# A decoder step on one core: the first conditioning section, loaded and computed in quarters

## The chip, the core and the metric

The kernel runs on one core of a Trainium2 chip. Its time is the device time of one execution in microseconds (us). TensorE (PE) multiplies, VectorE (DVE) and ScalarE (ACT) work on tiles, GpSimd (POOL) issues a few small transfers and SyncE (SP) issues nearly all the others. Each engine takes its instructions in the order in which they stand in its queue, and an instruction that waits holds up those behind it.

## What is computed

Two layers of a decoder trunk, for a prompt of 512 rows and for 8 samples of 4 rows, 544 columns in all once the rows are turned into columns. Cut to what the change touches:

```python
mod = jax.nn.silu(c) @ w + b                        # c: 1 + 8 rows of 1024; w: 1024 x 6144
sh_m, sc_m, g_m, sh_f, sc_f, g_f = split(mod, 6)    # six sections of 1024 features
hin = rmsnorm(x, norm_g[layer, 0]) * (1.0 + sc_m) + sh_m
gate_br, x_br = jnp.split(hin @ w_in, 2, axis=-1)   # first projection: 1024 -> 2 x 1536
```

So the first projection needs a scale (section 1 of the conditioning, `sc_m`) and a shift (section 0, `sh_m`) for each of the 1024 features of x, one vector for the prompt and one for each sample. Section 1 is the first section that the kernel computes.

## The kernel before, in words

x is held turned, `X[128 features, 8 chunks, 544 columns]`. Float32 products are made of three passes: each operand is cut into a high part (`hi`, `HH`) on ACT and a rest (`lo`, `HL`) on DVE, and TensorE adds hi*HH, hi*HL and lo*HH, each in two halves of 272 columns. One tile m of 128 output features over all 8 chunks k therefore takes 48 matmuls (line 119).

The stretch in question is the first 70 us. Its steps, with their lines:

- The conditioning vectors are loaded (`crow`), passed through silu and turned into `scT`. A half of a section (512 features) is four transfers of 512 KB (`ada_half_dma`, L461), 32 small float32 matmuls into four 32-column strips of TensorE (`ada_mm`, L580; the hardware runs each as two, so the trace counts 64), a copy to SBUF on ACT (`adas`, L588), one transpose (L590), and the addition of the bias (`ada_add`, L568). `ada_derive` (L573, L574) turns the scale into the multiplier that is applied to x.
- The norm gains and the biases come as 20 rows of 1024 (`r1`, L472 and L473) and are turned by eight transposes into `G1` (`g1_layout`, L562). `ada_add` and `ada_derive` read G1.
- x comes in four transfers of 256 features (`xrow`, L481). `x_layout(k)` turns two chunks (L531, copies on ACT and DVE, L532); `xs_layout` does the samples (L554). `x_sq` squares a chunk on ACT (L535).
- `hin_scaled` multiplies chunks of x by the multiplier and cuts them into HH and HL (L857, L860, L861, samples L434 and L435).
- The gate branch's first three tiles (`g0_mm`) are multiplied with these. The norm's factor R is not in yet; it is applied when the sum leaves PSUM (L946). R comes from `sums` and `mean_rstd` (L926, L932, L412 to L415) and needs the squares of all eight chunks.
- Section 0 (the shift) follows in two halves, `t_sh0` and `t_sh1`. With R and the shift, `hin_full` makes the full input for the x branch (L448, L452, L453), which is multiplied next, chunks 0 to 3 first and 4 to 7 then.

Before the change the first half of section 1 is computed, then chunks 0 to 3 of x are scaled and multiplied, then the second half and chunks 4 to 7. The squares, sums and R stand in the middle, so that tiles 1 and 2 of the gate branch are still to be multiplied when R is ready.

The program's order within each engine's queue is not the order of the source alone: a scheduler moves instructions forward or back between engines when it writes the queues, and the order is then fixed. Later loads and cuts are placed by a clock that counts matmuls (`Clock`, `Stream`). Weight and x tiles come from one pool of 16 buffers, and the PSUM tiles named `aux` from a pool of two.

## Time and profile before

| | |
|---|---|
| three runs | 1432.13, 1434.71, 1434.84 us (median 1434.71) |
| the profiled execution | 1435.27 us, of which the profile's span is 1433.5 us |
| mean granted TensorE clock | 0.989 of full speed |
| TensorE busy | 1395.7 us, 97% of the span |
| VectorE, ScalarE busy | 703.7 us (49%), 632.5 us (44%) |
| mean DMA rate | 116 GB/s over the span, 309 GB/s in the first fortieth |

A row of the profile gives the line of the kernel, the engine, the operation, output<-input by the program's names, partitions x elements, and a count. Busy time of TensorE counts pipelined matmuls and does not mean full speed. "Granted clock" is the share of 2.4 GHz that TensorE was given; 0.5 is 1.2 GHz.

### The profile page before, as it was taken

The page shows a single profiled execution, that of the slowest core. Times are in us where ns is not written, and L with a number is a line of the kernel's source. Part 1 is how long each engine was busy: PE and PEld are TensorE (multiplying, and loading weights), DVE is VectorE, ACT ScalarE, POOL GpSimd, SP SyncE. Part 2 cuts the span into 40 slices and gives each one's busy share as a digit, 9 for nine tenths or more (in the row PEclk, how much of TensorE's full clock was granted, in tenths as well). Part 3 has the DMA queues.
Part 4 walks back from the last instruction along what each step waited for, and adds up shares of the span by engine and source line. Part 5 has one row for each costly group of instructions (what it writes and reads, how often), then busy time and mean ns, then how long its engine had stood idle before and what let it go on. Part 6 is the DMA issues. An engine that isn't in the chain of part 4 may idle for free.

```text
span 1433.5 us, 27033 instructions
## 1 busy us (share of the span) xinstructions
PE 1395.7 (97%) x11472; PEld 1319.4 (92%) x11472; DVE 703.7 (49%) x1442; ACT 632.5 (44%) x1160; POOL 41.1 (3%) x76
## 2 busy tenths in 40 slices
PE   8999999998999999999998999999899999999997
PEld 6899989997999999999997989999899999999996
DVE  4767476779422332333349446653972233333334
ACT  4465746846523413414425434432573341432523
POOL 1200000000100000000000200000000000000000
PEclk8999999999999999999999999999999999999998
DMA  9554554321545545543221333122232222222201
GB/s 309 174 173 130 163 151 149 103 89 60 180 154 174 170 157 173 170 157 115 62 86 60 95 96 107 61 74 62 90 100 91 89 89 89 89 89 89 89 1 63
DMA packets 132227, 165.71 MB, mean 116 GB/s; under 512 B 10168, under 2 KB 111560, under 8 KB 132106
## 3 DMA queue, kind: packets, MB, share of 16 engines
q1 hardware_dynamic: 130346, 161.89, 35.9%
q0 software_dynamic: 1760, 2.09, 0.7%
q8 instruction: 90, 1.47, 0.4%
q14 instruction: 31, 0.25, 0.1%
HBM read 161.31 MB, written 2.65 MB: 114 GB/s over the span
## 4 chain that ended last, share of the span: by engine, by line
PE 65%; issue 26%; DVE 5%; ACT 2%; DMA 1%; POOL 0%; SPq 0%; POOLq 0%; ACTq 0%; DVEq 0%
PE acc L119 58%; PE aux L609 3%; DVE lo L182 1%; PE acc L1478 1%; DVE MIX L448 1%; DVE X L662 1%; DMA xsr<-in_x_sample_dram 1%; DVE HL L453 1%; PE aux L1397 0%; PE aux L580 0%; DVE MIX L660 0%; PE aux L390 0%; ACT HH L452 0%; DVE rs L414 0%; DVE R L415 0%
## 5 line engine op out<-in xcount | busy, mean ns | idle before, releaser
L119 PE MATMUL acc<-HH,hi 128*128 128x272 f32 x1776 | 399.2, 293 | 12.6 <-ACT HH L452 11.2
L119 PE MATMUL acc<-HH,lo 128*128 128x272 f32 x1776 | 394.0, 292 | 3.4 <-DVE lo L182 3.4
L182 DVE TENSOR_TENSOR lo<-raw,hi 128x512 fp32r<-128x512 f32 (+1 forms) x404 | 263.2, 682 | 254.3 <-ACT hi L181 188.1
L119 PE MATMUL acc<-HL,hi 128*128 128x272 f32 x1776 | 355.4, 289 | 3.5 <-DVE HL L453 3.1
L181 ACT CAST hi<-raw 128x512 fp32r<-128x512 f32 (+1 forms) x404 | 230.3, 613 | 281.7 <-PE acc L119 159.2
L119 PEld LDWEIGHTS acc<-HH,hi 128*128 128x128 f32 x1776 | 293.6, 191 | 23.2 <-ACT HH L452 13.7
L119 PEld LDWEIGHTS acc<-HH,lo 128*128 128x128 f32 x1776 | 293.1, 191 | 11.5 <-issue 6.7
L119 PEld LDWEIGHTS acc<-HL,hi 128*128 128x128 f32 x1776 | 273.5, 189 | 10.9 <-issue 5.4
L119 PE MATMUL acc<-hh,lo 128*128 128x272 f32 x1024 | 230.0, 290 | 0.0
L119 PE MATMUL acc<-hh,hi 128*128 128x272 f32 x1024 | 229.8, 290 | 0.0
L119 PE MATMUL acc<-hl,hi 128*128 128x272 f32 x1024 | 229.7, 290 | 0.0
L119 PEld LDWEIGHTS acc<-hh,hi 128*128 128x128 f32 x1024 | 168.0, 188 | 3.9 <-issue 3.8
L119 PEld LDWEIGHTS acc<-hh,lo 128*128 128x128 f32 x1024 | 168.1, 188 | 3.7 <-issue 3.6
L119 PEld LDWEIGHTS acc<-hl,hi 128*128 128x128 f32 x1024 | 168.1, 188 | 3.6 <-issue 3.5
L1267 DVE TENSOR_TENSOR hl<-hf,hh 128x544 fp32r<-128x544 f32 (+1 forms) x76 | 47.7, 634 | 175.2 <-ACT hh L1266 175.0
L1264 ACT ACTIVATE hf<-acc 128x544 f32<-128x544 f32 (+1 forms) x76 | 41.2, 550 | 128.1 <-PE acc L119 126.1
L710 DVE TENSOR_TENSOR MIX<-MIX,acc 128x544 f32<-128x544 f32 x44 | 31.6, 717 | 75.9 <-PE acc L119 75.9
L119 PE MATMUL acc<-hi,HH 128*128 128x256 f32 x192 | 54.8, 285 | 0.0
L119 PE MATMUL acc<-hi,HL 128*128 128x256 f32 x192 | 54.6, 284 | 0.0
L119 PE MATMUL acc<-lo,HH 128*128 128x256 f32 x192 | 53.8, 280 | 0.0
L119 PE MATMUL acc<-yh,hi 128*128 128x272 f32 x208 | 52.7, 291 | 0.3 <-ACT MIX L708 0.3
L119 PE MATMUL acc<-yh,lo 128*128 128x272 f32 x208 | 52.6, 291 | 0.0
(332 smaller groups left out, 1444.5 us busy)
## 6 DMA issues: line engine op xcount, KB each, us to landing
ada<-in_ada_w_dram SPq DMA_DIRECT2D x96, 512.0 KB, 4.9
raw<-in_mlp_w_up_dram SPq DMA_DIRECT2D x64, 512.0 KB, 4.3
raw<-in_mlp_w_down_dram SPq DMA_DIRECT2D x64, 512.0 KB, 4.5
raw<-in_lru_w_in_dram SPq DMA_DIRECT2D x24, 512.0 KB, 4.5
raw<-in_sg_w_in_dram SPq DMA_DIRECT2D x24, 512.0 KB, 4.6
raw<-in_sg_w_out_dram SPq DMA_DIRECT2D x12, 512.0 KB, 4.2
raw<-in_lru_w_out_dram SPq DMA_DIRECT2D x8, 384.0 KB, 3.0
raw<-in_lru_w_out_dram SPq DMA_DIRECT2D x6, 512.0 KB, 6.4
```

Source lines behind the costliest of these rows:

```text
L119: nc.tensor.matmul(out, lhsT, rhs, start=start, stop=stop)
L181: A.copy(h_, raw[:, c:c + st])
L182: V.tensor_tensor(l_, raw[:, c:c + st], f32(h_), op=ALU.subtract)
L448: V.scalar_tensor_tensor(wv, X[:, k, c0:c1], Am[:, k, 0:1], R[:, c0:c1], op0=ALU.mult, op1=ALU.mult)
L453: V.scalar_tensor_tensor(HL[:, k, c0:c1], wv, sh[:, k, 0:1], f32(HH[:, k, c0:c1]), op0=ALU.add, op1=ALU.subtract)
L609: nc.tensor.matmul(ps[32 * g:32 * g + 32, :], scT[:, k, :], ts_[g // 2][:, (g % 2) * 512:(g % 2) * 512 + 512], start=(k == 0), stop=(k == ...
L662: V.scalar_tensor_tensor(X[:, j, c0:c1], MIX[:, j, c0:c1], Gm[:, j, 0:1], X[:, j, c0:c1], op0=ALU.mult, op1=ALU.add)
L710: V.tensor_tensor(mv, mv, ps[:, :, 0:HW], op=ALU.add)
L1264: A.activation(dw, ps, AF.Relu)
L1267: V.tensor_tensor(dl, dw, f32(dh), op=ALU.subtract)
L1478: nc.tensor.matmul(ps[p0:p0 + 32, 0, ck * P:(ck + 1) * P], vp[ck // 2, c][:, o:o + 32], wT[g], start=True, stop=True, tile_position=(0, p0))
```

## The change

Section 1 is loaded and computed in four quarters of 256 features in place of two halves. `ada_quarter_dma` loads a quarter in two transfers of 512 KB, whose pieces in memory are 256 features (1 KB) long where those of a half were 512 features (2 KB). `ada_quarter` adds the even chunks of the 1024 inputs into two of the four strips and the odd ones into the other two, so that after the transpose the two partial results must be added: one more small operation on DVE for each quarter. The quarters' transfers alternate with those of x and of the first weights. The work on x, the multiplications of the gate branch and the cutting of its weights follow the quarters, two chunks of x with each; tiles 0 and 1 go first and tile 2 later. The sums and R come after the last quarter, all of the first shift half after that. `xs_layout` stands behind the first `x_layout`, and `g1_layout` ahead of the first quarter.

```diff
@@ -464,16 +464,24 @@
             ts.append(t_)
         return ts
 
+    def ada_quarter_dma(sec, q):
+
+        ts = [wtile("ada") for _ in range(2)]
+        for i, t_ in enumerate(ts):
+            nc.sync.dma_start(t_.rearrange("p (a n) -> p a n", a=4),
+                              ada_w[0, i * 512:i * 512 + 512, sec * D + q * 256:sec * D + q * 256 + 256]
+                              .rearrange("(a p) n -> p a n", p=P))
+        return ts
+
     crow = wtile("crow")
     nc.sync.dma_start(crow[0:1, :], c_prompt)
     nc.sync.dma_start(crow[1:9, :], c_sample)
-    t_sc0 = ada_half_dma(1, 0, n=2)
+    t_scq = [ada_quarter_dma(1, 0)]
     r1 = wtile("r1")[0:20, :]
     nc.sync.dma_start(r1[0:8, :], norm_g.rearrange("l j d -> (l j) d"))
     nc.sync.dma_start(r1[8:20, :], ada_b.rearrange("l (j d) -> (l j) d", d=D))
     xsr = wtile("xsr")[0:NSMP, :]
     nc.sync.dma_start(xsr, x_sample.rearrange("s t d -> (s t) d"))
-    ada_half_dma(1, 0, t_sc0, 2)
     xrow = []
 
     def x_dma(i):
@@ -483,12 +491,15 @@
     u0, u1 = ug0 = st.us[0:2]
     u0.spare = u1.spare = True
     x_dma(0)
+    u0.dma(4)
+    t_scq.append(ada_quarter_dma(1, 1))
     x_dma(1)
-    u0.dma(4)
     u1.dma()
+    t_scq.append(ada_quarter_dma(1, 2))
     x_dma(2)
+    st.load(("g", 0, 0))
+    t_scq.append(ada_quarter_dma(1, 3))
     x_dma(3)
-    t_sc1 = ada_half_dma(1, 1)
     st.load(("g", 0, 1))
     r2t = []
 
@@ -589,6 +600,24 @@
         pt = aux()
         nc.tensor.transpose(pt[:, 0:P], raw[:, 0:P], ident)
         ada_add(0, sec, 4 * half, 4, pt[:, 0:P].rearrange("p (g s) -> p g s", g=4)[:, :, 0:9])
+
+    def ada_quarter(sec, q, ts):
+
+        ps = aux()
+        for k in range(KD):
+            for j in range(2):
+                g = 2 * (k % 2) + j
+                c = (k % 4) * 256 + j * P
+                nc.tensor.matmul(ps[32 * g:32 * g + 32, 0:P], scT[:, k, :], ts[k // 4][:, c:c + P],
+                                 start=(k < 2), stop=(k >= KD - 2), tile_position=(0, 32 * g))
+        raw = slot("adas")
+        A.copy(raw[:, 0:P], ps[:, 0:P])
+        pt = aux()
+        nc.tensor.transpose(pt[:, 0:P], raw[:, 0:P], ident)
+        ptv = pt[:, 0:P].rearrange("p (r j s) -> p r j s", r=2, j=2)
+        ada_add(0, sec, 2 * q, 2, ptv[:, 0, :, 0:9])
+        m_ = MOD[0][:, sec, 2 * q:2 * q + 2, :]
+        V.tensor_tensor(m_, m_, ptv[:, 1, :, 0:9], op=ALU.add)
 
     def ada_gen(jobs, every):
         def load(l, blk, k):
@@ -871,23 +900,7 @@
             shift_split(sh0, k, 0, SEQ)
 
     K0, K1 = range(4), range(4, KD)
-    psa = aux()
-    ada_mm(psa, t_sc0, range(4))
-    fill(F2)
-    xs_layout()
     g1_layout()
-    ada_mm(psa, t_sc0, range(4, KD))
-    fill(F3)
-    ada_half(1, 0, t_sc0, psa)
-    x_layout(0)
-    u0.piece()
-    u1.piece()
-    x_layout(2)
-    fill(F4)
-    hin_scaled(0, 4)
-    u0.piece()
-    u1.piece()
-    V.tensor_tensor(MIX[:, :, SEQ:T], X[:, :, SEQ:T], X[:, :, SEQ:T], op=ALU.mult)
     accs = [acc() for _ in range(3)]
 
     def g0_mm(m, k):
@@ -897,26 +910,11 @@
             for h in (0, 1):
                 mm(accs[m][:, h, 0:HW], w[:, s], r[:, k, HS[h]], k == 0 and i == 0, k == KD - 1 and i == 2)
 
-    def g0_k(*ks):
-        for k in ks:
-            for m in range(3):
+    def g0_k(ms, *ks):
+        for m in ms:
+            for k in ks:
                 g0_mm(m, k)
 
-    t_sh0 = ada_half_dma(0, 0)
-    st.load(("x", 0, 1))
-    t_sh1 = ada_half_dma(0, 1)
-    load_vec()
-    g0_k(0, 1)
-    x_layout(4)
-    x_layout(6)
-    g0_k(2)
-    u0.piece()
-    u0.piece()
-    ada_half(1, 1, t_sc1)
-    hin_scaled(4, KD)
-    g0_k(3)
-    for k in range(KD):
-        x_sq(k)
     sq = slot("p0")[:, 0:T].rearrange("p (h n) -> p h n", h=2)
 
     def sums(h):
@@ -932,25 +930,58 @@
         nc.tensor.matmul(pst[:, 0:HW], dmean, sq[:, h], start=True, stop=True)
         rstd(R[:, HS[h]], pst[:, 0:HW])
 
+    ada_quarter(1, 0, t_scq[0])
+    x_layout(0)
+    xs_layout()
+    hin_scaled(0, 2)
+    u0.piece()
+    V.tensor_tensor(MIX[:, :, SEQ:T], X[:, :, SEQ:T], X[:, :, SEQ:T], op=ALU.mult)
+    g0_k((0, 1), 0, 1)
+    ada_quarter(1, 1, t_scq[1])
+    x_layout(2)
+    hin_scaled(2, 4)
+    u0.piece()
+    u1.piece()
+    g0_k((0, 1), 2, 3)
+    t_sh0 = ada_half_dma(0, 0)
+    st.load(("x", 0, 1))
+    t_sh1 = ada_half_dma(0, 1)
+    load_vec()
+    ada_quarter(1, 2, t_scq[2])
+    x_layout(4)
+    hin_scaled(4, 6)
+    u0.piece()
+    g0_k((2,), 0, 1, 2, 3)
+    g0_k((0, 1), 4, 5)
+    ada_quarter(1, 3, t_scq[3])
+    x_layout(6)
+    hin_scaled(6, KD)
+    u0.piece()
+    u1.piece()
+    for k in range(KD):
+        x_sq(k)
+    g0_k((2,), 4, 5)
     gts, xbs, xcs, xhs, xls, yhs, yls = {}, {}, {}, {}, {}, {}, {}
     ux0 = st.us[st.ix["x", 0, 0]:][:2]
     ux0[0].spare = True
+    g0_k((0,), 6, 7)
+    sums(0)
+    g0_k((1,), 6)
+    sums(1)
+    g0_k((1,), 7)
+    mean_rstd(0)
+    g0_k((2,), 6)
+    mean_rstd(1)
+    g0_k((2,), 7)
+    for _ in range(4):
+        ux0[0].piece()
+    psa = aux()
+    ada_mm(psa, t_sh0, range(KD))
     for m in range(3):
-        for k in K1:
-            g0_mm(m, k)
-            if m == 0 and k < 6:
-                sums(k - 4)
-            elif m == 0:
-                mean_rstd(k - 6)
         gts[m] = slot("gt")
         V.tensor_tensor(gts[m][:, 0:T].rearrange("p (h n) -> p h n", h=2), accs[m][:, :, 0:HW],
                         R.rearrange("p (h n) -> p h n", h=2), op=ALU.mult)
         if m == 0:
-            for _ in range(4):
-                ux0[0].piece()
-            psa = aux()
-            ada_mm(psa, t_sh0, range(KD))
-        if m == 1:
             ada_half(0, 0, t_sh0, psa)
             hin_full(0, 4)
     for i in range(2):
```

On TensorE the program begins as follows, before (`r` are the rows of gains and biases, `ada` the conditioning weights, `xsr` and `xrow` the rows of the samples and of x):

```order
L522 MATMUL aux_138<-fill_136,dmean 128x512 x4
L548 MATMUL aux_154<-ident,crow_98 128x9 x8
L580 MATMUL aux_165<-ada_101,scT 32x128 x8
L580 MATMUL aux_165<-ada_103,scT 32x128 x8
L554 MATMUL aux_182<-ident,xsr_108 128x32 x8
L562 MATMUL aux_192<-ident,r_4_105 128x20 x8
L580 MATMUL aux_165<-ada_110,scT 32x128 x8
L580 MATMUL aux_165<-ada_112,scT 32x128 x8
L590 MATMUL aux_220<-ident,adas_218 128x128
```

and after the change:

```order
L533 MATMUL aux_138<-fill_136,dmean 128x512 x4
L559 MATMUL aux_154<-ident,crow_98 128x9 x8
L573 MATMUL aux_165<-ident,r_4_105 128x20 x8
L611 MATMUL aux_179<-ada_101,scT 32x128 x8
L611 MATMUL aux_179<-ada_102,scT 32x128 x8
L616 MATMUL aux_198<-ident,adas_196 128x128
L542 MATMUL aux_202<-ident,xrow_110 128x128 x4
L542 MATMUL aux_208<-ident,xrow_110 128x128 x4
L565 MATMUL aux_214<-ident,xsr_108 128x32 x8
L119 MATMUL acc_175<-HH,hi_233 128x272
```

The transposes of the gains and biases now stand ahead of every conditioning matmul, and half as many of those stand ahead of the first matmul of the projection.

On DVE the second quarter's chain now reads (`lo` are the rests of weight tiles, `HSM` the samples; L579 and L620 are the two additions, L584 and L585 the multiplier):

```order
L579 TENSOR_TENSOR MOD_95<-aux_281,G_164 128x18
L620 TENSOR_TENSOR MOD_95<-MOD_95,aux_281 128x18
L182 TENSOR_TENSOR lo_307<-raw_112,hi_306 128x512
L584 SCALAR_TENSOR_TENSOR MOD_95<-MOD_95,G_164 128x18
L182 TENSOR_TENSOR lo_311<-raw_120,hi_310 128x512
L543 COPY X<-aux_291 128x512
L585 TENSOR_SCALAR MOD_95<-MOD_95 128x18
L886 TENSOR_TENSOR HSM<-X,MOD_95 128x64
L435 TENSOR_TENSOR HL<-HSM,HH 128x2x32
L890 SCALAR_TENSOR_TENSOR HL<-X,MOD_95,HH 128x512 x2
```

where the second half's chain had been:

```order
L568 TENSOR_TENSOR MOD_95<-aux_443,G_164 128x36
L573 SCALAR_TENSOR_TENSOR MOD_95<-MOD_95,G_164 128x36
L574 TENSOR_SCALAR MOD_95<-MOD_95 128x36
L857 TENSOR_TENSOR HSM<-X,MOD_95 128x128
L861 SCALAR_TENSOR_TENSOR HL<-X,MOD_95,HH 128x512
L435 TENSOR_TENSOR HL<-HSM,HH 128x4x32
L861 SCALAR_TENSOR_TENSOR HL<-X,MOD_95,HH 128x512 x3
```

Two cuts of weights and a copy of x now stand inside the chain that makes the multiplier. It is so for the fourth quarter too; in the third they stand outside.

Behind the second of the two means for R, TensorE's queue now reads, up to the x branch (`acc_177` is tile 2 of the gate branch, `ada_338` to `ada_358` are the shift's weights, `acc_704` the x branch's first tile):

```order
L119 MATMUL acc_177<-HH,hi_524 128x272 x2
L119 MATMUL acc_177<-HL,hi_524 128x272 x2
L119 MATMUL acc_177<-HH,lo_525 128x272 x2
L591 MATMUL aux_634<-ada_338,scT 32x128 x8
L591 MATMUL aux_634<-ada_340,scT 32x128 x8
L591 MATMUL aux_634<-ada_342,scT 32x128 x8
L591 MATMUL aux_634<-ada_344,scT 32x128 x8
L601 MATMUL aux_671<-ident,adas_669 128x128
L591 MATMUL aux_755<-ada_352,scT 32x128 x8
L591 MATMUL aux_755<-ada_354,scT 32x128 x8
L591 MATMUL aux_755<-ada_356,scT 32x128
L119 MATMUL acc_704<-HH,hi_618 128x272
```

Between the second mean and the first matmul of the x branch there stand six matmuls of the projection; before there were 48 (tiles 1 and 2 over chunks 4 to 7). In place of the others stand the shift's matmuls, of both halves. Behind the first 280 of TensorE's some 6,400 rows, and behind the first 250 of DVE's, the queues of before and after hold the same instructions in the same order.

## Rows read from the trace of the kernel before

**Rows 1.** The page, parts 1 and 2: busy time, then tenths in 40 slices, TensorE clock granted.

```profile
PE 1395.7 (97%) x11472; PEld 1319.4 (92%) x11472; DVE 703.7 (49%) x1442; ACT 632.5 (44%) x1160; POOL 41.1 (3%) x76
...
PEclk8999999999999999999999999999999999999998
```

**Rows 2.** The chain of waits, 0 to 60 us: start, length, what the end hangs on.

```profile
3.61 7.68 DMA xsr<-in_x_sample_dram
...
13.64 1.91 PE aux L580 x32
...
22.37 5.55 PE acc L119 x30
...
45.25 0.45 DVE R L415
...
51.23 0.74 ACT HH L452
...
52.01 0.51 PE acc L119 x2
```

**Rows 3.** The same chain, 52 to 110 us.

```profile
59.56 1.48 PE aux L580 x46
...
62.92 2.76 PE acc L119 x20
65.68 0.49 PE aux L510 x6
66.17 8.42 PE acc L119 x66
```

**Rows 4.** Timeline of PE: start, length, line, tiles, count, in brackets idle and releaser.

```profile
9.12 0.64 PE L580 MATMUL aux<-ada,scT 128*32 128x128 f32 x16 [0.19 <-DMA ada<-in_ada_w_dram]
11.42 0.66 PE L554 MATMUL aux<-ident,xsr 32*128 32x32 f32 x8 [1.66 <-DMA xsr<-in_x_sample_dram]
12.60 1.04 PE L562 MATMUL aux<-ident,r 20*128 20x20 f32 x8 [0.52 <-DVE X L555]
16.16 3.57 PE L531 MATMUL aux<-ident,xrow 128*128 128x128 f32 x16
20.81 0.82 PE L119 MATMUL acc<-HH,hi 128*128 128x272 f32 x3 [1.09 <-ACT hi L181]
32.07 1.95 PE L580 MATMUL aux<-ada,scT 128*32 128x128 f32 x64
36.03 0.27 PE L590 MATMUL aux<-ident,adas 128*128 128x128 f32 x1
43.14 0.62 PE L932 MATMUL aux<-p,dmean 128*128 128x272 f32 x2
```

**Rows 5.** Timeline of the DMA queue SP: when an issue started and how long it took.

```profile
2.91 0.66 SPq L473 DMA_DIRECT2D r<-in_ada_b_dram  x1
3.61 0.81 SPq L475 DMA_DIRECT2D xsr<-in_x_sample_dram  x1
4.46 1.17 SPq L461 DMA_DIRECT2D ada<-in_ada_w_dram  x2
```

**Rows 6.** DMA issues of 0 to 40 us: count, KB each, median us to landing.

```profile
raw<-in_lru_w_in_dram SPq DMA_DIRECT2D x6, 512.0 KB, 10.7
xrow<-in_x_prompt_dram SPq DMA_DIRECT2D x4, 512.0 KB, 8.8
```

**Rows 7.** Timeline of ACT and DVE, one row for each kind of step.

```profile
15.57 0.27 ACT L588 COPY adas<-aux 128x128 f32<-128x128 f32 x1 [7.51 <-PE aux L580]
16.40 0.20 DVE L568 TENSOR_TENSOR MOD<-aux,G 128x36 f32<-128x36 f32 x1 [2.40 <-PE aux L590]
17.25 0.59 ACT L532 COPY X<-aux 128x512 f32<-128x512 f32 x1 [1.42 <-PE aux L531]
17.87 0.72 ACT L860 ACTIVATE HH<-X,MOD 128x512 fp32r<-128x512 f32 x1
18.11 0.69 DVE L532 COPY X<-aux 128x512 f32<-128x512 f32 x1 [1.06 <-PE aux L531]
20.56 0.29 DVE L857 TENSOR_TENSOR HSM<-X,MOD 128x128 f32<-128x128 f32 x1
20.89 0.30 ACT L434 CAST HH<-HSM 128x128 fp32r<-128x128 f32 x1
21.43 0.68 DVE L182 TENSOR_TENSOR lo<-raw,hi 128x512 fp32r<-128x512 f32 x1
```

**Rows 8.** Windows of 2 us: length, five engines' busy time, then PEclk, DMA share, GB/s.

```profile
14.00:16.00 2.00, 1.61 (x31) 1.09 (x22) 0.00 (x1) 0.27 (x1) 0.00 (x0) 0.50 1.10 349
16.00:18.00 2.00, 2.00 (x10) 1.78 (x11) 0.57 (x3) 0.71 (x2) 0.00 (x0) 0.50 1.13 325
20.00:22.00 2.00, 1.19 (x6) 0.84 (x6) 1.90 (x4) 1.87 (x5) 0.00 (x0) 1.00 1.10 354
24.00:26.00 2.00, 2.00 (x11) 2.00 (x10) 1.54 (x3) 1.54 (x3) 0.00 (x0) 0.50 1.05 386
```

**Rows 9.** Two windows of PE alone: length, busy, matmuls, PEclk, DMA share, GB/s.

```profile
23.10:26.40 3.30, 3.30 (x18) 0.54 1.05 387
...
56.20:59.50 3.30, 3.30 (x30) 1.00 0.00 0
```

## The prediction, made before the changed kernel had run

> **What bounds the kernel now.** I read the page first: TensorE is busy for 97% of the span and was granted full speed in nearly all of its 40 slices, the first one excepted [rows 1]. Then the chain of waits over the first 60 us. It begins on transfers and small steps, and only from 22.4 us on does it lie on the projection's matmuls [rows 2]; behind 66 us it is matmuls almost throughout [rows 3]. So the kernel is bound by TensorE behind 66 us, where the order is the same in both kernels, and what the change is worth is how much earlier or later TensorE comes to that place, the first matmul of the x branch on chunks 4 to 7, at 66.17 us.
>
> Then the timeline, for what holds up TensorE until then. It waits for the second conditioning tile until 9.12, for the samples' rows until 11.4, and starts the projection at 20.81 [rows 4]. From there it has work until 52.01, when the x branch starts; R is complete at 45.7, and 48 matmuls of the gate branch cover the steps from R to the x branch's first input [rows 2]. The last gap is at 59.6 to 62.9, where the second shift half is multiplied late and the chain runs over its copy and sums [rows 3]. From the x branch's start to 66.17 it is 14.1 us.
>
> **How the new queue runs.** I follow the new queues of TensorE, DVE and ACT by hand: a step starts when its engine is free and its inputs are there, and lasts what its row says. For the order of before this gives 51.8 us for the x branch's start, where the trace has 52.0. A projection matmul in a full stream costs 8.42/66 = 0.128 us [rows 3]. TensorE at full clock first, the clock afterwards.
>
> *First quarter.* It needs 1 MB where the half needed 2 MB, but the transposes of the gain and bias rows stand in front of it. Their landing has no row. They are issued at 2.91, directly ahead of the samples' rows, whose landing ends a wait at 11.29, and behind the tiles that landed by 9.12 [rows 2, 4, 5]. They land between 9.1 and 11.3; a queue that serves 12 and 32 rows of 4 KB alike speaks for the late end, and I take 11.2. Before, TensorE met this wait behind that of the samples, where it cost nothing. Then 0.66 for eight transposes (as the samples' eight took [rows 4]), 0.98 for 32 conditioning matmuls (half of 1.95 for 64 [rows 4]): 12.9. Copy 0.27, transpose 0.3, x's copy 0.59, HH 0.72, the weights' cut 0.6 [rows 4, 7]: the projection starts at 16.0, 4.8 us before 20.81. x has landed by then: its first transfer is issued where a conditioning tile was, at 4.46 [rows 5], plus 8.8 [rows 6] is 13.3. The last x transfer takes the 20th place of the queue, where before a weight tile was issued at about 20 and took 10.7 [rows 6]: 31 with some loss for shorter pieces, and it is needed at 37. Transfers do not bound the later quarters.
>
> *Later quarters.* From the last conditioning matmul of a quarter to the first HH of its chunks the chain is: copy and transpose 0.75 with the hand-overs, two additions 0.4, two cuts of weights 1.2, the copy of x 0.7, multiplier 0.2, samples 0.25 on DVE and on ACT (0.29 and 0.30 for twice the chunks), HH 0.7 [rows 7]: 4.5 us. In the third the cuts are out of it: 3.3. TensorE has beside it eight transposes (0.9), 12 matmuls of tile 2 (1.5) and 0.8 to 1.3 of conditioning or sums, some 3.5, and so stands for about 1.0 to 1.5 in each. The quarters' last conditioning matmuls then come at 21.1, 26.6 and 35.9. The second half's had come at 34.0 [rows 4]. The lead of 4.8 us is gone.
>
> *R and the x branch.* HH of chunk 6 at 40.5, then 36 matmuls (4.6), half of the sums and two means with their hand-overs (2.0): the second mean ends at 47.1 where it ended at 43.8 [rows 4]. R follows in 1.9 as before: 49.0, 3.3 later. From R to the x branch's first input before were 6.3 us [rows 2], with two evacuations of gate tiles in the chain on DVE, one of which (0.64) is now behind it: 5.6, so the x branch starts at 54.6. Behind the second mean TensorE now has 6 matmuls, the first shift half (1.95) and a bit more than half of the second (1.0), and stands for about 4 us.
>
> *What comes back.* That work is then done. From the x branch's start to the place at 66.17 there remain 72 matmuls (9.2), 30 of the 64 conditioning instructions (0.9), one block of small transposes (0.5 [rows 3]), and about 0.5 of waits: 11.1 instead of 14.1. The second shift half's sums now lie beside the x branch's matmuls. The place comes at 54.6 + 11.1 = 65.7, that is 0.4 earlier.
>
> *Clock.* Before, the granted clock was 0.50 in 14 to 18 us, after TensorE had waited for the samples and while it ran conditioning matmuls and transposes; it was 1.00 at 20 to 22, where TensorE was busy for 1.19 of 2 us, and 0.50 again at 24 to 26 [rows 8]. A stretch of 3.3 us at 0.54 held 18 matmuls where one at 1.00 held 30: 12 x 0.128 = 1.5 us lost [rows 9]. The new queue stands from 8.0 to 11.2, so its first quarter too runs at the lower level; carried through the steps this moves R by 0.9 to 1.4, and I take 1.0. And the x branch now starts behind 4 us of standing and 3 us of conditioning matmuls, more of both than ahead of the drop at 24: I take the drop as likely, for one such stretch of 1.5 us and at times two: 1.7.
>
> The Trainium skill, in "TensorE: Matmul & The Clock Gate", section "Loop structure matters more than you think", speaks against this change: bursts of matmuls with waits between them run cold, dense ones stay warm. The drop behind 20 to 22 us agrees [rows 8]. By that rule the sum is +2.3, without it +0.6.
>
> *Sum.* -0.4 + 1.0 + 1.7 = +2.3 us. On the profiled execution (1435.27, of which 1433.5 is span) that is 1437.6; that execution lay 0.56 above the median of the runs, 1434.71, and for the median I say 1434.7 + 2.3 = 1437.0.
>
> Costed at nothing: the four additions on DVE (in the chains above, and else beside TensorE's work); the second shift half's transfers, of which one waits until tile 2's weights are cut (about 38 us) for its buffer and which then land, at 8 to 11 us [rows 6], near 48, needed from 50 (if they take 3 us more the x branch starts that much later); POOL's loads, which wait for buffers of the third quarter that come free near 31 and 38, about as before.
>
> **The rivals.**
>
> *Faster.* The gain and bias rows land at 9.5 and TensorE takes the quarter at once. For it: only bounds are known. Against it: they queue with the samples' rows, at 11.29. The steps then give an x branch at 53.1 and -1.9; if x is a microsecond early as well, -2.9. With a clock that holds, 1431.8 to 1432.8; take 1432.3.
>
> *The clock holds at the x branch.* Everything else as forecast: -0.4 + 1.0 = +0.6, or 1435.3. For it: conditioning matmuls may hold the clock, as they did not break it at 32 to 34 us, amid other matmuls. Against it: 14 to 18 us.
>
> *Slower, by the clock in the quarters.* The quarters' transposes and conditioning matmuls, with the short waits, leave the clock at the lower level until the projection's chunks 4 and 5, near 36 us. Half of TensorE's work in that stretch lies on the chain between quarters; carried through the steps the x branch starts 6 to 7 us later: 1441. It decides when two stretches on end of the three between 20 and 36 us stay low. Against it: before, transposes alone filled 16.2 to 19.7, and the clock was at 1.00 in 20 to 22 [rows 4, 8].
> The Trainium skill, same page, section "Part 4: PE-mode transpose", says that transposes do not count as TensorE's being busy in the way that raises the clock; by it this rival would be the likely one, at 1441. The rise behind 16.2 to 19.7 us disagrees [rows 4, 8].
>
> **How the numbers follow.** Forecast 0.45 (its own range 1435.4 to 1439.2), clock holds 0.20, faster 0.22, slower by the clock 0.13. A measurement of this kernel can tell 0.2%, or 2.9 us, from no change: 1431.8 to 1437.6. Faster holds a little over half of its rival and a rest of the others: 0.17. Slower holds all of the last rival and just under half of the forecast's range, and a rest: 0.35. Within: 0.48. The range is 1431.9 to 1440.8; a tenth lies on either side, in the faster and the slower rival.
>
> **What would show it.** In the changed kernel's timeline, line 573 waits until about 11.2 with TensorE idle from 8.0; the projection starts at 16 to 17.3; R (line 415) is complete at 49 to 51; the first matmul on `HH` behind the shift's comes at 54.6 to 56.5, with some 3 us of idle ahead of it; the granted clock is near 0.5 in a stretch behind that; the gap at 60 to 63 is gone. The prediction is wrong in its first step if line 573 starts before 10, in its middle if R is complete before 47, in its clock term if the clock is 1.00 from 52 to 62, and in its frame if the time of the place at 66.17 and the kernel's time do not move together.

## The result and the profile after

The changed kernel took 1442.09 us (median of four runs, 1440.27 to 1443.96), the kernel before 1434.18 in the same session (1432.13 to 1434.84): 1.0055 times as long, 95% interval 1.0043 to 1.0067. That is 7.9 us slower, and outside the forecast's range. The profiled execution took 1440.27 us, 1438.5 of it span: 5.0 us more than the profiled span of before. It was the fastest of the four runs, and the profiled execution of before (1435.27) was slower than any of its four, so the two traces show some 5 of the 7.9 us.

Busy times and clock on the page read as before [rows 1]; the loss is too small to show in shares of the span.

```profile
PE 1398.2 (97%) x11474; PEld 1318.2 (92%) x11474; DVE 704.8 (49%) x1456; ACT 633.9 (44%) x1164; POOL 41.1 (3%) x76
...
PEclk8999999999999999999999999999999999999998
```

The chain of waits of the changed kernel, 0 to 75 us (start, length, what the end hangs on), which answers to [rows 2, 3]:

```profile
2.98 7.16 DMA r<-in_ada_b_dram
...
11.29 1.91 PE aux L611 x32
...
16.81 0.82 PE acc L119 x2
17.63 0.99 PE aux L611 x10
18.62 1.21 PE acc L119 x4
19.83 0.54 PE aux L611 x6
20.37 2.46 PE acc L119 x18
22.83 0.62 PE aux L611 x16
...
25.82 0.57 PE aux L611 x16
...
27.58 0.55 PE aux L611 x10
28.13 0.70 PE acc L119 x4
28.83 0.35 PE aux L611 x6
29.18 2.96 PE acc L119 x22
...
34.39 0.34 PE aux L611 x2
...
35.17 0.57 PE aux L611 x16
...
36.44 0.35 PE aux L611 x8
...
39.25 0.38 PE aux L611 x6
...
43.77 1.05 PE aux L924 x16
...
51.24 0.47 PE aux L930 x2
...
53.20 0.04 DVE R L415
...
58.34 0.73 ACT HH L452
...
59.12 0.60 PE acc L119
59.72 1.43 PE aux L591 x22
...
72.37 0.50 PE aux L521 x6
72.86 2.19 PE acc L119 x16
```

The projection starts at 16.81, 4.0 us earlier than before. From there to 51.71 the chain is TensorE's nearly throughout: conditioning (L611) in stretches of 2 to 16 between the projection's matmuls (L119), and the sums (L924). The second mean (L930) ends at 51.71 instead of 43.8, and the x branch starts at 59.12 instead of 52.01. The place, the first L119 behind the block of six small transposes (L521, L510 before), comes at 72.86 instead of 66.17.

The timeline of PE shows where TensorE stood; it answers to [rows 4]:

```profile
10.28 1.01 PE L573 MATMUL aux<-ident,r 20*128 20x20 f32 x8 [1.88 <-DMA r<-in_ada_b_dram]
...
23.79 0.33 PE L616 MATMUL aux<-ident,adas 128*128 128x128 f32 x1 [0.39 <-ACT adas L614]
...
39.97 0.33 PE L616 MATMUL aux<-ident,adas 128*128 128x128 f32 x1 [0.38 <-ACT adas L614]
...
54.98 0.33 PE L601 MATMUL aux<-ident,adas 128*128 128x128 f32 x1 [0.65 <-ACT adas L599]
...
59.12 0.60 PE L119 MATMUL acc<-HH,hi 128*128 128x272 f32 x1 [2.61 <-ACT HH L452]
```

Behind the second and the fourth quarter's conditioning it stood for 0.4 us each, then for 0.65 us behind the shift's first half and for 2.61 us ahead of the x branch. Windows with the granted clock next to the end (0.50 is 1.2 GHz, 1.00 is 2.4), which answer to [rows 8]:

```profile
14.00:16.00 2.00, 2.00 (x13) 1.58 (x11) 0.94 (x5) 1.06 (x2) 0.00 (x0) 0.50 1.10 348
...
20.00:22.00 2.00, 2.00 (x19) 1.70 (x14) 0.00 (x0) 0.00 (x0) 0.00 (x0) 0.95 1.11 350
...
56.00:58.00 2.00, 0.51 (x14) 0.24 (x6) 2.00 (x4) 0.00 (x0) 0.00 (x0) 0.94 1.05 364
58.00:60.00 2.00, 0.88 (x9) 0.63 (x13) 2.00 (x6) 1.66 (x4) 0.00 (x0) 0.50 1.13 327
...
62.00:64.00 2.00, 2.00 (x15) 1.62 (x12) 2.00 (x5) 1.91 (x4) 0.85 (x1) 0.50 0.00 0
...
66.00:68.00 2.00, 2.00 (x19) 2.00 (x18) 1.36 (x3) 0.00 (x0) 0.00 (x0) 1.00 0.47 102
```

In windows of 0.1 us the clock is low from 10.0 to 20.2 us, and again from 57.7 to 64.6: it fell while TensorE stood for the gain and bias rows, and the second time during the standing of 2.61 us. In the trace of before it is low from 12.5 to 19.4 and from 22.7 to 26.1, 10.3 us in all against 17.0.

**A measure of progress.** Blocks move about in the order, so one block's start is a rough marker. In what follows I also count the matmuls of line 119 done in the first 300 us (length, busy time, count, clock, DMA share, GB/s). Before:

```profile
0.00:300.00 300.00, 248.34 (x1879) 0.98 0.54 169
```

After:

```profile
0.00:300.00 300.00, 243.95 (x1834) 0.97 0.54 166
```

The changed kernel is 45 matmuls behind, at 0.125 us each 5.6 us. It is 48 behind at 70 us already, and at 200 us 44: the loss arises ahead of 70 us. Some records may be missing in each trace, so I read differences of under 8 matmuls (1 us) as nothing. The count and the times don't always agree: the count is of one execution, the times of several.

### The profile page after: what moved, and what is told of

Same layout as the page of the kernel before. It is cut to its first block, busy times and chain, and to the rows that moved or that the text cites. A ratio compares the mean times of both kernels' runs of the same rounds, so it can differ in the third digit from the quotient of the medians.

```text
span 1438.5 us, 27057 instructions
## 1 busy us (share of the span) xinstructions
PE 1398.2 (97%) x11474; PEld 1318.2 (92%) x11474; DVE 704.8 (49%) x1456; ACT 633.9 (44%) x1164; POOL 41.1 (3%) x76
## 3 DMA queue, kind: packets, MB, share of 16 engines
q8 instruction: 90, 1.47, 0.4%
## 4 chain that ended last, share of the span: by engine, by line
PE 65%; issue 26%; DVE 6%; ACT 2%; DMA 0%; POOL 0%; SPq 0%; POOLq 0%
PE acc L119 58%; PE aux L638 3%; DVE lo L182 1%; PE acc L1509 1%; DVE MIX L448 1%; DVE HL L453 1%; DVE X L691 1%; PE aux L611 0%; DMA r<-in_ada_b_dram 0%; PE aux L1428 0%; DVE MIX L689 0%; PE aux L390 0%; PE aux L542 0%; DVE rs L414 0%; PE aux L1434 0%
## 5 line engine op out<-in xcount | busy, mean ns | idle before, releaser
L119 PE MATMUL acc<-HH,hi 128*128 128x272 f32 x1776 | 398.0, 293 | 13.2 <-ACT HH L452 13.1
L119 PE MATMUL acc<-HH,lo 128*128 128x272 f32 x1776 | 391.7, 291 | 3.1 <-DVE lo L182 3.1
L119 PE MATMUL acc<-HL,hi 128*128 128x272 f32 x1776 | 355.6, 289 | 3.3 <-DVE HL L453 3.3
L119 PEld LDWEIGHTS acc<-HH,hi 128*128 128x128 f32 x1776 | 292.1, 190 | 24.3 <-ACT HH L452 15.7
L119 PEld LDWEIGHTS acc<-HH,lo 128*128 128x128 f32 x1776 | 291.2, 190 | 11.7 <-issue 6.9
L119 PEld LDWEIGHTS acc<-HL,hi 128*128 128x128 f32 x1776 | 273.5, 188 | 11.0 <-issue 6.0
L119 PE MATMUL acc<-hh,lo 128*128 128x272 f32 x1024 | 229.8, 290 | 0.0
L119 PE MATMUL acc<-hh,hi 128*128 128x272 f32 x1024 | 229.7, 290 | 0.0
L119 PE MATMUL acc<-hl,hi 128*128 128x272 f32 x1024 | 229.4, 289 | 0.0
L119 PEld LDWEIGHTS acc<-hh,lo 128*128 128x128 f32 x1024 | 168.1, 188 | 3.7 <-issue 3.6
L119 PEld LDWEIGHTS acc<-hh,hi 128*128 128x128 f32 x1024 | 167.9, 188 | 3.9 <-issue 3.8
L119 PEld LDWEIGHTS acc<-hl,hi 128*128 128x128 f32 x1024 | 168.1, 188 | 3.6 <-issue 3.6
L119 PE MATMUL acc<-hi,HH 128*128 128x256 f32 x192 | 54.7, 285 | 0.0
L119 PE MATMUL acc<-hi,HL 128*128 128x256 f32 x192 | 54.5, 284 | 0.0
L119 PE MATMUL acc<-lo,HH 128*128 128x256 f32 x192 | 53.8, 280 | 0.0
L119 PE MATMUL acc<-yh,hi 128*128 128x272 f32 x208 | 52.6, 290 | 0.3 <-ACT MIX L737 0.3
L119 PE MATMUL acc<-yh,lo 128*128 128x272 f32 x208 | 52.5, 291 | 0.0
```

Of the source, the lines that this page charges most:

```text
L119: nc.tensor.matmul(out, lhsT, rhs, start=start, stop=stop)
```

## Experiments

Three theories. A: the sums and means come too late, so that little work lies beside the chain from R to the x branch. B: the quarters make TensorE's own work longer. C: the lower clock. The ratio is to the kernel before, with its 95% interval; the second mean's start is from the timeline of PE, in us; the count is line 119's in 0 to 300 us. The changed kernel was timed in its first session alone; each variant was timed beside the kernel before in a later one.

| run | ratio [interval] | second mean starts | count |
|---|---|---|---|
| before | 1 | 43.14 | 1879 |
| changed | 1.0055 [1.0043, 1.0067] | 51.08 | 1834 |
| e1_cover | 1.0027 [1.0017, 1.0037] | 50.16 | 1840 |
| e2_sums_first | 1.0013 [1.0004, 1.0022] | 47.96 | 1864 |
| e3_fill | 1.0047 [1.0034, 1.0060] | 51.06 | 1839 |
| e4_half1 | 1.0038 [1.0024, 1.0051] | 50.34 | 1845 |
| e5_loads | 1.0006 [0.9997, 1.0014] | 44.47 | 1885 |
| e6_order | 1.0034 [1.0021, 1.0047] | 50.61 | 1832 |
| e7_first_half | 1.0004 [0.9993, 1.0015] | 45.86 | 1865 |
| e8_fill_wait | 1.0049 [1.0037, 1.0061] | 50.27 | 1837 |
| e9_half_fill | 0.9993 [0.9984, 1.0001] | 42.64 | 1891 |
| e10_before_fill | 0.9995 [0.9986, 1.0004] | 41.63 | 1891 |
| e11_rows_later | 0.9997 [0.9989, 1.0006] | 43.00 | 1891 |
| e12_twice | 1.0061 [1.0047, 1.0075] | 54.49 | 1811 |
| e13_sums_fill | 1.0006 [0.9997, 1.0015] | 45.97 | 1880 |
| e14_later_fill | 0.9993 [0.9984, 1.0002] | 42.00 | 1899 |

**Loads or order.** e5 takes the new loads with the order of before (`ada_qq` is before's `ada_mm`, reading quarters). Its edit, cut, against the kernel before:

```diff
-    t_sc0 = ada_half_dma(1, 0, n=2)
+    t_scq = [ada_quarter_dma(1, 0)]
...
-    ada_mm(psa, t_sc0, range(4))
+    ada_qq(psa, t_scq[0:2], range(4))
...
-    ada_half(1, 1, t_sc1)
+    psb = aux()
+    ada_qq(psb, t_scq[2:4], range(KD))
+    ada_half(1, 1, None, psb)
```

> The new loads alone: section 1 in quarters of 256 features (1 KB pieces), in the changed kernel's order of transfers, but the first half computed when its two quarters are there, and everything else computed in the order of before. Theory of TensorE's work (the loss is the longer and interrupted work of the quarters): the queue of before is back, only its first half lands later, since x's first transfer and the first projection's weights stand ahead of the second quarter (about 1 MB and 0.5 MB at 350 GB/s, 3 to 4 us); the projection starts at 24, the x branch at 53 to 55 and the time is 1435 to 1437. Theory of the loads (1 KB pieces and the order cost the time): 1440 or more, most of the 7 us.

e6 takes the loads of before with the new order, each quarter reading its columns out of the half. This edit and the following ones are against the changed kernel, and are cut where `...` stands:

```diff
-    t_scq = [ada_quarter_dma(1, 0)]
+    t_sc0 = ada_half_dma(1, 0, n=2)
...
+    ada_half_dma(1, 0, t_sc0, 2)
...
+    t_sc1 = ada_half_dma(1, 1)
...
+    t_scq = [t_sc0, t_sc0, t_sc1, t_sc1]
```

> The new order of computing alone: quarters of the conditioning section, taken out of the tiles of before, whose loads and their order are those of before. Theory of TensorE's work: the same queue as the changed kernel, conditioning instructions at 0.057 us instead of 0.037 and three more stops for a copy; the x branch starts near 59 and the place (the first block of small transposes behind it, 65.6 before, 72.3 in the changed kernel) comes at 71 to 73, 1440.5 to 1442. Theory of the loads: the place comes at 67 or before, 1436.

The loads alone cost nothing that can be measured; the projection started at 23.21, and yet the x branch's small transposes came at 65.61 as before. The order alone cost 0.34%, and its count, 1832, is the changed kernel's. So the loss that the trace shows is one of the order; in times 0.34 of 0.55% are, with intervals that overlap, and what makes up the rest is not shown.

**Theory A.** e1 puts tile 2 behind the means:

```diff
-    g0_k((2,), 4, 5)
...
-    g0_k((0,), 6, 7)
+    g0_k((0,), 6)
     sums(0)
-    g0_k((1,), 6)
+    g0_k((0,), 7)
     sums(1)
-    g0_k((1,), 7)
+    g0_k((1,), 6)
     mean_rstd(0)
-    g0_k((2,), 6)
+    g0_k((1,), 7)
     mean_rstd(1)
-    g0_k((2,), 7)
+    g0_k((2,), 4, 5, 6, 7)
```

> The same work; the sums of squares and the two means stand between tiles 0 and 1 of the first projection on chunks 6 and 7, and all of tile 2 on chunks 4 to 7 (24 matmuls) behind them, where it can lie beside the chain from the mean to the x branch. Theory A (the loss is that the second mean comes last, at 51.7 us, with little left to do beside the chain from it to the x branch): 18 matmuls of 0.125 us leave the queue ahead of the mean, so it ends at 49.5, R is complete at 51.4, the x branch starts at 56.9 instead of 59.1, and the time is 1439.9 against the changed kernel's 1442.1 (0.3% over before). Theory B (the loss is TensorE's own work, which the quarters made longer): TensorE has as much to do and the x branch still starts near 59; no change, 1442. Theory C (the loss is the lower clock): if TensorE no longer stands before the x branch, the stretch of lower clock from 58 to 65 us goes, the x branch takes 11.1 instead of 13.7 us to its chunks 4 to 7, and the time is 1437.5 with A and C together.

e2 puts the squares and sums ahead of the last quarter:

```diff
-    ada_quarter(1, 3, t_scq[3])
+    for k in range(6):
+        x_sq(k)
     x_layout(6)
+    for k in range(6, KD):
+        x_sq(k)
+    ada_quarter(1, 3, t_scq[3])
...
-    g0_k((0,), 6, 7)
     sums(0)
-    g0_k((1,), 6)
+    g0_k((2,), 4)
     sums(1)
-    g0_k((1,), 7)
+    g0_k((2,), 5)
     mean_rstd(0)
-    g0_k((2,), 6)
+    g0_k((0,), 6)
     mean_rstd(1)
-    g0_k((2,), 7)
+    g0_k((0,), 7)
+    g0_k((1, 2), 6, 7)
```

> The same work; the transposes of x's chunks 6 and 7 and the squares stand ahead of the last quarter's conditioning matmuls, and the sums and means ahead of the projection on chunks 4 to 7 of all but a few tiles. Theory A (the mean came too late): the second mean ends near 45 us, R is complete near 47, the x branch starts when TensorE has done the projection and the shift's matmuls, near 54.5, its place at 67, and the time is about 1436.5, within 0.3% of before. Theory B (TensorE's own work got longer by some 4 us with the quarters): the mean moves as said, but TensorE still ends the projection at 52.4 or later, the x branch starts no earlier than 54.5 and the time stays 2 to 3 us over before. Theory C (lower clock alone): the early stretch to 20.5 us is untouched, so some 2 us of the loss stay, 1436 to 1440.

e1's mean came only 0.9 us earlier, less than A's 2.25, since its first quarter also began 0.9 us later: the gain and bias rows landed at 11.3 there, at 10.1 in the changed kernel's profile. Counted from the start of the rows' transposes, the mean came 2.1 us earlier, near A's figure. The standing ahead of the x branch fell from 2.61 to 1.61 us and the stretch of lower clock from 6.8 to 3.4 us. Its times fell by 0.28%, 4.0 us, where the count rose by no more than 6. Timeline of e1:

```profile
58.20 0.39 PE L119 MATMUL acc<-HH,hi 128*128 128x272 f32 x1 [1.61 <-ACT HH L452]
```

e2's mean came 3.1 us earlier, TensorE stood for 0.33 us ahead of the x branch, and the clock held there. Timeline of e2:

```profile
40.68 1.08 PE L611 MATMUL aux<-ada,scT 128*32 128x128 f32 x32 [0.24 <-ACT X L543]
...
47.96 0.62 PE L930 MATMUL aux<-p,dmean 128*128 128x272 f32 x2
...
56.66 0.39 PE L119 MATMUL acc<-HH,hi 128*128 128x272 f32 x1 [0.33 <-ACT HH L452]
```

Its count:

```profile
0.00:300.00 300.00, 246.17 (x1864) 0.98 0.53 168
```

30 of the 45 matmuls are back, and in times 6.0 of 7.9 us (0.42% of 1434). A holds for the most part. The x branch started at 56.66, not at A's 54.5: the rest is something else, as B and C had it.

But e2 changes more than the place of the sums. Its queue has the last quarter's conditioning in one stretch (32 in 1.08 us, where the changed kernel took 1.64 in four). And its x branch started 2.5 us earlier than the changed kernel's while its place came 4.9 us earlier, so half of the gain at the place arose behind the x branch's start, where the clock now held. The late sums lead to the standing and the standing goes with the lower clock; no run holds the clock there with the sums left late, so how much each is worth by itself is not shown.

**Theory B.** e4 loads and computes the second half in one:

```diff
-    ada_quarter(1, 2, t_scq[2])
+    ada_half(1, 1, t_sc1)
     x_layout(4)
...
-    ada_quarter(1, 3, t_scq[3])
     x_layout(6)
```

> The changed kernel with the second half of the section loaded and computed in one, as before the change (64 conditioning matmuls in one or two stretches of the queue instead of 64 in seven); quarters 0 and 1 stay. Theory B (small conditioning matmuls in between the projection's cost 0.057 us each where they cost 0.030 in one stretch, and the first matmul behind each such stretch costs some 0.2 us more): the last conditioning matmul and all behind it come 1.7 to 2.5 us earlier, the mean at 49.5, the time 1440. Theories A and C: the half must land as a whole, so chunks 4 and 5 come later; the mean stays near 51.7 and the time at 1442.

e12 does every quarter's conditioning twice:

```diff
-        for k in range(KD):
+        for k in [*range(KD), *range(KD)]:
             for j in range(2):
```

> The changed kernel with every quarter's 32 conditioning matmuls done twice over, the second time in place of the first (128 more in all). Theory of TensorE's work (TensorE has no wait to spare from 16.8 to 52 us, so that what the quarters add to its queue is added to the time): some 1.9 us in the first quarter at the lower clock and 1.0 us in each other, 4.5 to 5 us in all; the place comes at 76 to 77 and the time is 1446 to 1447. Theory of the chains (TensorE stands for 1.0 to 1.5 us in each quarter for copies, cuts and HH, as my forecast had it): these waits take up most of it in quarters 1 to 3, and the time is 1443.5 to 1444.5.

e4 brought the mean 0.7 us earlier instead of 1.7 to 2.5, and 0.17% of time. In its profile the rows' transposes began at 11.22, 0.9 us later than in the changed kernel's; counted from there the mean came 1.7 us earlier, at the lower edge of B's range. So some of B holds, though not all that e4 gained is B's: its clock at the x branch was low for 3.4 us instead of 6.8.

In e12 the second mean came 3.4 us later, its small transposes L521 2.6 us later (74.85), and the count fell by 23, 2.9 us. The expectation had the added work too dear: up to the place TensorE's conditioning took 14.6 us instead of 12.5, so 128 more matmuls cost 2.1 us and not 4.5 to 5. They stood in stretches of up to 64, and the first quarter had 3.4 us less of the lower clock. What was added did pass to the mean and to the place, so TensorE had no waits to take it up, as B has it. The times rose from 1.0055 to 1.0061 alone, within the intervals and below both expectations, and don't decide.

Count of e12:

```profile
0.00:300.00 300.00, 241.00 (x1811) 0.98 0.53 164
```

**Theory C.** e3 puts fillers into two waits of the first quarter:

```diff
         A.copy(raw[:, 0:P], ps[:, 0:P])
+        fill(4 if q == 0 else 0)
         pt = aux()
...
+    fill(4)
     g1_layout()
```

> The changed kernel with 8 more filler matmuls (128x512, on zeros): four ahead of the transposes of the gain and bias rows, where TensorE waited 1.9 us, and four behind the first quarter's conditioning matmuls, where it waited 0.4 us. Theory C (the lower clock from 10.3 to 20.5 us costs): the granted clock stays at 1.00 over that stretch or comes back sooner, the first quarter's projection takes 0.125 us a matmul at once, the last of the projection comes 1.5 to 2 us earlier and the time is 1440.3. Theories A and B (late mean, longer work): no change or 0.5 to 1.5 us more for the fillers themselves, 1442 to 1443.5.

e8 puts them into the first alone:

```diff
+    fill(4)
     g1_layout()
```

> The changed kernel with four filler matmuls only in the wait for the gain and bias rows (0.5 us each at full clock, in a wait of 1.9 to 3.6 us). Theory of the lower clock: it stays at 1.00 from 8 to 21 us; the first quarter's conditioning takes 1.1 instead of 1.9 us, eight transposes 1.25 instead of 1.9, the first quarter's matmuls half; the projection starts at 15.5 to 16.5, R comes 2 to 3 us earlier, and the time is 1439 to 1440. Theory that the clock of the first quarter is worth nothing (transfers or DVE and ACT set the pace of the quarters): R stays near 53.6 and the time at 1441 to 1442.

e13 has the same edit on top of e2:

> All four quarters, the sums ahead of the last quarter, and four filler matmuls in the wait for the gain and bias rows. What e2 still lost against before, 15 projection matmuls or 1.9 us by 300 us, is either the lower clock from 11 to 21.5 us or the number of conditioning stretches between the projection's matmuls (eight instead of two). If the clock: it stays at 1.00, some 15 matmuls come back, and the time is that of before or 1 us less, 1433 to 1435. If the stretches: no more than 0.5 us comes back and the time stays at 1436.

Windows of the changed kernel and, below it, of e8 (length, busy, matmuls, clock, DMA share, GB/s):

```profile
10.30:20.50 10.20, 9.72 (x80) 0.51 1.11 335
```

```profile
10.30:20.50 10.20, 8.90 (x95) 1.00 1.11 331
```

The fillers hold the clock at 1.00. In e3 eight of them put off the projection's start by 3.1 us (19.88), and the mean came at the same time: with the clock held, the stretch between took 3.1 us less. But the fillers take time themselves. Timeline of e8, where each filler counts as two matmuls:

```profile
8.23 1.98 PE L533 MATMUL aux<-fill,dmean 128*128 128x512 f32 x4
...
10.48 1.98 PE L533 MATMUL aux<-fill,dmean 128*128 128x512 f32 x4
12.40 0.67 PE L573 MATMUL aux<-ident,r 20*128 20x20 f32 x8
```

Four took 3.8 us from start to start where the expectation had 2, and the rows' transposes began at 12.40 instead of 10.28. From there to the second mean e8 took 37.9 us and the changed kernel 40.8. Of these 2.9 us, 2.1 went into the later start: the mean came 0.8 us earlier. TensorE again stood for 2.61 us ahead of the x branch, the clock fell there as before, and the count rose by 3. With the sums ahead of the last quarter the same fillers gave 16 matmuls, in e13:

```profile
0.00:300.00 300.00, 247.22 (x1880) 1.00 0.54 169
```

With that the four quarters are level with before in count (1880 to 1879) and in time (1.0006 [0.9997, 1.0015]). That e13 gained more than e8 is for the most part the rows' landing: without fillers the rows' transposes began at 10.28 in the changed kernel's profile and at 11.10 in e2's, with them at 12.40 and 12.15. From the transposes to the mean the held clock gave 3.0 us in e13 (33.8 for e2's 36.9), about as much as in e8.

**Is an early first quarter a gain?** e7 keeps quarters in the first half and takes before's order from chunk 4 on:

```diff
-    ada_quarter(1, 2, t_scq[2])
+    g0_k((2,), 0, 1)
     x_layout(4)
-    hin_scaled(4, 6)
...
-    ada_quarter(1, 3, t_scq[3])
     x_layout(6)
...
+    ada_half(1, 1, t_sc1)
+    hin_scaled(4, KD)
+    g0_k((0, 1, 2), 3)
```

> Quarters for the first half alone; the second half is loaded and computed in one, and from x's chunks 4 to 7 on the order is that of before (sums between the matmuls of the first tile, tiles 1 and 2 behind them). Theory of late sums and TensorE's work together: three of the seven conditioning stretches go, the sums come some 8 us earlier and are covered again by 48 matmuls; the second mean ends at 42 to 44, the x branch starts at 51 to 53, the place comes at 65 to 67, and the time is 1434 to 1436, as before. If it is faster than before by 1 us or more, the early first quarter is a gain by itself that the changed kernel lost later. Theory of the lower clock: the early stretch from 10 to 21 us is as in the changed kernel, so some 2 us of the loss stay: 1437.

e9 is e7 with e8's edit:

> Quarters for the first half only and the order of before from chunks 4 to 7 on, and four filler matmuls in the wait for the gain and bias rows. If the lower clock from 10 to 24 us is what remains of the loss there: the granted clock stays at 1.00, the projection starts at 16.5 to 17.2, the second mean ends near 44, the x branch starts at 53.5 and its place comes at 65.5 instead of 67.3; time 1432.5 to 1433.5, 1 to 2 us faster than before. If TensorE's work behind the second half alone counts: 1434 to 1435.

e11 is e7 with the rows' transposes behind the first quarter's conditioning:

```diff
+        if q == 0:
+            g1_layout()
         raw = slot("adas")
...
-    g1_layout()
```

> Quarters for the first half only, and the transposes of the gain and bias rows behind the first quarter's conditioning matmuls, so that TensorE no longer waits for these rows ahead of the first quarter. My forecast had that wait as a cost of 2 to 3 us at the start. If the start counts: conditioning begins at 9.5 to 10.5 instead of 12.2, the projection at 16.5 instead of 18.0, and the time is 1433 to 1433.5. If the start is worth nothing (the lead is spent before the second half in any case): 1434 to 1435.

e14 is e11 with fillers:

```diff
+    fill(3)
     ada_quarter(1, 0, t_scq[0])
```

> Quarters for the first half only, the gain and bias rows behind the first quarter, and three filler matmuls in the wait for the first quarter's tiles. Both single steps brought the kernel to 12 projection matmuls ahead of before. If they add up, the clock is 1.00 throughout the first 60 us, the projection starts at 15 to 15.5, and the time is 1432 to 1432.5, 0.15 to 0.2% faster than before. If the start is worth nothing once the clock holds, since the second half's tiles set the pace from there: 1433.5.

e10 is the kernel before with fillers in its own wait:

```diff
-    F1, F2, F3, F4 = 4, 0, 0, 0
+    F1, F2, F3, F4 = 4, 3, 0, 0
```

> The kernel before with three filler matmuls in its own wait for the samples' rows (1.7 us). If holding the clock is worth something for any order: conditioning and 16 transposes at 13.6 to 19.7 take 3.3 instead of 5.5 us and the projection starts at 18.7 instead of 20.8; the second half's transfers land as before, so the mean comes at most 1 us earlier and the time is 1433 to 1434.5. If transfers bind the second half: no change, 1434.4.

e7 is as fast as before in time, and 14 matmuls behind it. e9, e11 and e14 are 12 to 20 matmuls ahead of before, and 0.03 to 0.07% faster in time, which the intervals don't tell from no change. Three fillers in the kernel before, without any quarters, give 12 as well:

```profile
0.00:300.00 300.00, 248.16 (x1891) 1.00 0.54 169
```

e10's projection starts at 21.25, 4.8 us behind e14's, and its second mean comes at 41.63, earlier than e14's 42.00. An early start of the projection is no gain here. A held clock gives 12 matmuls or 1.5 us in the order of before (e10), 16 in e2's (e13) and 26 in e7's (e9), and in times no more than 0.11%.

e10 also gives a fairer measure for e13, as the kernel before lost matmuls to its own low clock. With the clock at 1.00 in both, the four quarters of e13 are 11 matmuls or 1.4 us behind the two halves of e10, and their conditioning up to the place took 9.8 us against 8.5. The two differ in loads and order as well, but the 1.35 us of conditioning is nearly the whole distance; in times (1.0006 and 0.9995) the intervals overlap. No version beats before by what can be measured. e14 has the lowest median, 1433.09 beside 1434.57.

## Why the prediction was wrong

The sign was right, and the size fell short: +2.3 us forecast, +7.9 measured. With its clock terms in, the forecast put the place at 65.7 + 2.7 = 68.4; it came at 72.86. Of the 4.5 us between, 3.6 lie ahead of the second mean (51.71, where the forecast had 47.1 and 1.0 for the clock) and 0.9 between the x branch's start and the place (13.7, where it had 11.1 and 1.7). Of the 3.6, some 2 are a first-quarter clock that was mis-sized (below), the rows' early landing takes 1.1 off, and the rest, an estimate of 2.7, is the later quarters' work. The frame held: place and time moved the same way, the place by 6.7 us and the times by 7.9 (the profiled span by 5.0), in e2 the place by 1.8 and the time by 1.9. The order, not the loads, cost the time, as far as the runs tell (e5, e6).

What held: the rows' wait ahead of the first quarter (they landed at 10.14 to 11.36 us in the runs, 11.2 forecast); R 1.5 us behind the mean for 1.9; 5.9 us from R to the x branch for 5.6; the gap of before at 60 to 63, gone; the drop of the clock at the x branch. The end of the first quarter's conditioning (13.20 for 12.9) and the projection's start (16.81, within 16 to 17.3) came out by luck in part: in the profile the rows landed 1.1 us early, and the transposes and conditioning behind them took 1.3 us more, at the lower clock. The terms listed for the projection's start also add up to 15.4 and not 16.0; the transposes of x are not among them.

**The step that failed is "Later quarters", and with it the term of -0.4 us.** It gave 34.2 us from the first quarter's conditioning to the second mean (12.9 to 47.1), of which 1.0 to 1.5 us of standing in each quarter, on a chain of small steps on ACT and DVE. (For the third quarter its own figures, 3.3 us of chain beside 3.5 of work, leave no standing.) Measured were 38.5 us (13.20 to 51.71); of the 4.3 more, 1.6 to 1.9 are the clock (by e8 and e13), for which the sum had a term of its own. R was complete at 53.2, outside the 49 to 51 that I had named as the sign. TensorE stood for 0.39 us behind the second quarter, 0.38 behind the fourth and not at all behind the third. The path lay on TensorE's own queue, what I had called a wait was work, and so the second mean came 4.6 us late:

- Conditioning. I took 0.98 us for 32, half of 64 in one stretch. Split among the projection's matmuls, in stretches of 2 to 16, a quarter's took 0.99 + 0.54 + 0.62 = 2.15 us (the first 16 of it at the lower clock), then 1.47 and 1.64: 5.3 us for what three times 0.98, 2.9, would be.
- Matmuls behind such a stretch. Four took 0.70 us where 0.128 each makes 0.51, and I priced every one at 0.128. This is no loss against before: summed from start to start in the timelines, the gate branch's 144 took 22.3 us in either kernel.

Against before it is the conditioning that got dearer. Summed in the same way up to the place, its 256 matmuls took 9.4 us before, 12.5 in the changed kernel, 11.3 in e2 and 9.8 in e13. So of 3.1 us, 1.5 go with the clock of the first quarter (e2 to e13) and 1.2 with the clock at the x branch and the fewer stretches of e2. TensorE's idle time up to the place, summed over the timeline's brackets, rose by 0.9 us only, from 7.1 to 8.0: nearly all of the 6.7 us is work that took longer. For the splitting alone there are e4 (64 of the matmuls in two stretches: 11 matmuls or 1.4 us back, some of it by the clock) and, with the clock held, e13 beside e10 (1.4 us).

That the sums come last, the forecast had, and had it too cheap, as all that was mispriced stands ahead of them. e2 moves them, with what follows for the clock and the last quarter's stretches, and 6.0 of 7.9 us are back (30 of 45 matmuls).

**The clock at the x branch** was mis-sized: 1.7 us forecast as one stretch and at times two. It was as long as two (6.8 us at 0.50, where before had 3.4 behind 22.7): x branch to place took 13.7 us where e2, with the clock at 1.00, took 11.3 to the same matmul (56.66 to 68.0). That is 2.4 us, a little of it for eight conditioning matmuls fewer in e2.

**The first quarter's clock**, 1.0 us in the sum, was too small: held, it gave 2.9 us up to the mean in e8 and 3.0 in e13, less the time of the fillers 0.8 and 2.0. The rival of a low clock up to 36 us did not occur: the clock was at 1.00 from 20.2. Nor did the faster rival, though the rows landed at 10.1 in the profile, more than halfway to its 9.5: the mean came 4.6 us behind the forecast's 47.1 all the same.

The page of the Trainium skill whose rule on loops I weighed ("TensorE: Matmul & The Clock Gate", section "Loop structure matters more than you think") points the right way: TensorE stood and the clock fell, at 10.0 and at 57.7 us. That is no small part of the loss: half of what e2 gains at the place lies where its clock held, and e13 adds 16 matmuls by the clock alone. But not every wait had it: in e10 TensorE stood for 1.60 us at 19.6 to 21.2, and the clock stayed at 1.00.

What stays open: the changed kernel's profiled execution shows 5.0 us, its times 7.9, and there is no trace of its longer executions. And the late sums and the clock at the x branch are not told apart.

## What to carry to other kernels

Splitting a step to start the next one sooner moves the start of the chain; ask first what its end waits for. Here the end was the mean, which needs only x, and the new order put it behind the last quarter; with it moved ahead of that quarter, most of the loss was gone. And price small blocks of matmuls as they will stand in the queue, split and between others, not by their share of one long stretch.

## What had not been expected of the hardware

Two things. At the x branch the clock held behind 0.3 to 0.6 us of standing (e2, e7, e9), and fell with 1.61 (e1) and 2.61 (changed kernel, e3, e4, e6, e8, e12). With 2.61 it stayed low for 3.4 us in three of these runs (e3, e4, e12) and for 6.8 in the others. Elsewhere the length of the standing does not tell: the clock held through 1.60 us in e10 (timeline below), and it fell at 19.3 us in e12, where no wait since 14.5 us had been longer than 0.6.

```profile
21.25 0.64 PE L119 MATMUL acc<-HH,hi 128*128 128x272 f32 x3 [1.60 <-ACT hi L181]
```

And blocks of 32-column conditioning matmuls have a price for each stretch more than for each matmul, in the changed kernel at full clock, by the chain: 2 in 0.34 us, 6 in 0.35, 10 in 0.55, 16 in 0.57. Before has 64 in one stretch in 1.88 us (its chain, first row), and e12 has 62 in 1.95 (its timeline, second row):

```profile
32.14 1.88 PE aux L580 x64
```

```profile
41.06 1.95 PE L611 MATMUL aux<-ada,scT 128*32 128x128 f32 x62
```
